# Filter spectra with their even/odd sum and difference formed by TensorE, one store per side, and the second layer's modulation blocks emitted between the filter pairs

## The chip, the core and the metric

The kernel is one program on 1 core of a Trainium2 chip. The time is device microseconds (us) of that core for one execution. Engines are named as in the profile: PE is TensorE's matmul, PEld its weight load, DVE VectorE, ACT ScalarE, POOL GpSimd, and SP the engine that issues most DMAs.

## What is computed

A two-layer trunk over 1024 tokens of width 1024 with a context of 256 tokens. Layer 0 mixes neighbourhood attention and a gated DeltaNet, layer 1 is an order-2 Hyena block. Three pieces of the reference lie around the change. The modulation vectors of both layers come from the conditioning alone, and the filters of layer 1 come from a small network alone, so both are computed at the very start, beside layer 0's input:

```python
def adaln_in(s, cvec, norm_g, mod_w, mod_b):
    m = jax.nn.silu(cvec) @ mod_w + mod_b
    shift, scale, gate = jnp.split(m, 3, axis=-1)
    return rmsnorm(s, norm_g) * (1.0 + scale) + shift, gate

def long_conv(u, h_fwd, h_bwd, skip):
    ...
    hf = jnp.fft.rfft(h_fwd, n=n, axis=0)
    hb = jnp.fft.rfft(h_bwd, n=n, axis=0)
    ...

def hyena_layer(...):
    h, gate = adaln_in(s, cvec, norm_g, mod_w, mod_b)
    ...
    filt = hyena_filters(s.shape[1], fw1, fb1, ff1, fw2, fb2, ff2, fw3)
    z = x1 * long_conv(v, filt[:, 0, 0], filt[:, 0, 1], skip[0])
    y = x2 * long_conv(z, filt[:, 1, 0], filt[:, 1, 1], skip[1])
```

## The kernel before

`start` (L328) is the first stage. It makes the filters' hidden layer, the eight shift and scale blocks of layer 0's modulation (`mod_block`, tiles em_w, em_ps, em_t), and then loops over 8 column blocks `cb`. Each round calls `filter_pair`, which makes four filters of 1024 samples for 128 channels (matmuls into fh, L1280 and L1281; DVE multiplies them by a decay at L1282; ACT squares and scales them). For each of the two orders it then runs `filter_block` one step late through `flush(0)`, and `filter_spectrum` another step late through `flush(1)`. There are so 16 spectra, and they are called filters 1 to 16 here.

`filter_block` adds and subtracts the forward and the backward filter (fp on POOL at L1304, fh on DVE at L1305) and folds the result into short pieces: ft_sd, ft_d and ff, on POOL and DVE, L1139 to L1160 and L1318. PE transposes the pieces (fx_ps, L121), and ACT copies them to fx.

`filter_spectrum` (L1323) multiplies the pieces by small DFT matrices. It does so for two sides, the sine side 1 first and then the cosine side 0. On each side the even and the odd half of the coarse piece are two matmuls of 128x256 into one PSUM tile e (profile name fb). ACT copies the even half to t (profile name fo, L1340), and DVE forms sum and difference of the two halves (L1341, L1342) in the staging tile G. DVE then adds and subtracts a second PSUM tile r to a part of that result (L1343, L1344), and ACT copies the rest of r (L1345). G holds both sides and has one buffer. When side 0 is done, two stores take it to g_d: 1 MB at L1350 and 64 KB at L1351. PSUM tiles e, r and b2 share three buffers.

Beside the filters the stage has work that a scheduler places: at `cb` 0 the code emits, with a priority below all other work, the four gate blocks of layer 0's modulation, the first halves of eight gate projections (`zblock`, PE tiles z, 24 matmuls each, 192 in all) and all twelve blocks of layer 1's modulation (j = 0 to 11). Each modulation block loads two pieces of 512 KB (om_w, L208), makes 8 matmuls into a PSUM tile om_ps, and copies it by ACT to om_p. Blocks 0 to 7 are then transposed (om_t) and reduced by DVE; blocks 8 to 11, the gate part, take a one-row matmul (om_g, L224), an addition on DVE (L227) to a row loaded for it (om_gr, L226), and a store of that row (gate_d, L228). The PSUM pool of om_ps, om_t, om_g and z has one buffer. The weights of z and of the modulation go through the same three tags, wraw, whi and wlo, with two buffers each, so that a load waits for the matmuls of six pieces earlier.

After the loop `layer0_in` transposes the second half of the tokens (xtp, L401). `load_ab` loads the small weights wab through wraw as well, and `project` begins: 48 small matmuls (ab, L574) and then the large projections (dn, L110 to L112) with weights wdn.

A scheduler sets the order of the instructions of each engine from the program, its dependencies, its own costs and the priorities; on the chip each engine then runs its list in that order. SP's list is a queue too: an issue that waits for a buffer holds what stands behind it.

## Time and profile before

| | us |
|---|---|
| median of 3 runs | 1918.72 (1909.53 to 1919.75) |
| profiled execution, its own time | 1915.67 |
| span of the profile | 1913.7 |
| granted TensorE clock, mean | 0.953 |
| PE, DVE, ACT, POOL busy | 1743.7, 1379.5, 853.8, 624.6 |
| mean DMA rate | 142 GB/s |

The busy times are sums over stages with different limits. The first stage ends where the first dn matmul starts, 387 us into the span. Within it the 16 stores at L1350 mark the ends of the filters: the first is issued at 96.3 us, the twelfth at 324.8 us and the last at 377.4 us.

### The profile page before, as it was taken

Reading aid. Unit: us, or ns where it says so; the run is one execution under the profiler, and the core shown is the slowest. Engines: PE = TensorE matmul, PEld = TensorE weight load, DVE = VectorE, ACT = ScalarE, POOL = GpSimd, SP = SyncE. Lnnn points to the kernel's source line nnn. Section 1 sums busy time; section 2 is a strip of 40 time slices with the busy share of each in tenths; the row PEclk is TensorE's granted clock in tenths of the full one; section 3 lists DMA queues with packets and bytes.
Section 4 is the critical chain, followed back from the end, with each engine's and each line's share of the span. In section 5 each row is a group of like instructions: output and inputs, shape, how many; then the busy total and the mean of one; then the engine's idle time right before and its main releaser. Section 6 shows DMA issues by size and latency. Waiting matters only on the chain. (4 is left out here: it accounts for less than half of the span.)

```text
span 1913.7 us, 30399 instructions
## 1 busy us (share of the span) xinstructions
PE 1743.7 (91%) x11156; PEld 1422.0 (74%) x11156; DVE 1379.5 (72%) x2786; ACT 853.8 (45%) x1851; POOL 624.6 (33%) x878
## 2 busy tenths in 40 slices
PE   6798988799987998999988999888999999999998
PEld 2466755688876786888866787677888888888776
DVE  5999988657648544655565665748898998898666
ACT  5566564445525342333343544544344444444421
POOL 0755554412395767811044301420000000000310
PEclk9799978899999998999998999999999999999999
DMA  8445544313434367534389854533442443444424
GB/s 303 162 131 142 171 159 160 121 45 108 142 104 122 128 202 230 174 103 158 142 236 236 233 172 105 181 94 81 111 121 72 101 124 81 123 111 112 126 104 135
DMA packets 132080, 271.05 MB, mean 142 GB/s; under 512 B 43946, under 2 KB 65978, under 8 KB 129883
## 3 DMA queue, kind: packets, MB, share of 16 engines
q1 hardware_dynamic: 122330, 233.45, 37.8%
q0 software_dynamic: 9600, 35.66, 9.9%
q8 instruction: 88, 1.44, 0.3%
q14 instruction: 62, 0.50, 0.1%
HBM read 193.03 MB, written 76.03 MB: 141 GB/s over the span
## 5 line engine op out<-in xcount | busy, mean ns | idle before, releaser
L116 PE MATMUL hx<-h1h,w1x_hi 128*128 128x512 f32 x256 | 101.2, 395 | 0.0
L112 PE MATMUL dn<-hh,wdn_lo 128*128 128x512 f32 (+1 forms) x256 | 95.6, 375 | 5.9 <-POOL wdn_lo L105 5.9
L116 PE MATMUL hx<-h1l,w1x_hi 128*128 128x512 f32 x256 | 100.9, 394 | 0.0
L652 DVE SCALAR_TENSOR_TENSOR dacc<-dpad,convw,dacc 128x1024 f32<-128x1024 f32 (+1 forms) x80 | 83.8, 1078 | 23.6 <-ACT dacc L650 19.3
L116 PE MATMUL hx<-h1h,w1x_lo 128*128 128x512 f32 x256 | 100.7, 393 | 0.0
L111 PE MATMUL dn<-hl,wdn_hi 128*128 128x512 f32 (+1 forms) x256 | 95.2, 372 | 0.0
L110 PE MATMUL dn<-hh,wdn_hi 128*128 128x512 f32 (+1 forms) x256 | 95.2, 372 | 0.0
L757 POOL TENSOR_TENSOR Xb<-Xb,sub 80x31 f32<-80x31 f32 (+15 forms) x124 | 86.3, 696 | 8.4
L755 POOL TENSOR_TENSOR sub<-Lb,Xb 80x31 f32<-80x31 f32 (+15 forms) x124 | 76.0, 613 | 35.0 <-DMA Lb<-lsc_d 21.0
L1051 ACT ACTIVATE pr<-pr,st 128x640 f32<-128x640 f32 (+1 forms) x64 | 51.4, 802 | 63.6 <-DVE st L1050 63.5
L112 PEld LDWEIGHTS dn<-hh,wdn_lo 128*128 128x128 f32 x256 | 49.1, 192 | 14.7 <-POOL wdn_lo L105 6.1
L1171 ACT COPY fx<-fx_ps 128x512 f32<-128x512 f32 (+1 forms) x96 | 43.5, 483 | 28.4 <-PE fx_ps L121 24.9
L116 PE MATMUL hu<-h1h,w1u_lo 128*128 128x512 f32 x128 | 51.3, 401 | 4.7 <-DMA w1u_lo<-in_w 4.7
L110 PEld LDWEIGHTS dn<-hh,wdn_hi 128*128 128x128 f32 x256 | 49.2, 192 | 7.8
L121 PE MATMUL fx_ps<-ident,ff 128*128 128x128 f32 x288 | 49.9, 300 | 5.6 <-ACT fx L1171 3.6
L111 PEld LDWEIGHTS dn<-hl,wdn_hi 128*128 128x128 f32 x256 | 49.0, 192 | 8.0 <-issue 0.5
L116 PEld LDWEIGHTS hx<-h1h,w1x_lo 128*128 128x128 f32 x256 | 48.1, 188 | 9.0
L116 PEld LDWEIGHTS hx<-h1h,w1x_hi 128*128 128x128 f32 x256 | 48.2, 188 | 8.9
L116 PEld LDWEIGHTS hx<-h1l,w1x_hi 128*128 128x128 f32 x256 | 48.1, 188 | 8.9
L156 POOL DMA_DIRECT2D w1x_lo<-in_w x16 | 13.8, 864 | 124.8 <-ACT w1x_lo L154 116.7
L1280 PE MATMUL fh<-fhh,w3s 128*128 128x512 f32 x64 | 37.2, 584 | 16.6 <-DVE fh L1282 16.5
L116 PE MATMUL hu<-h1h,w1u_hi 128*128 128x512 f32 x128 | 51.5, 402 | 0.8 <-ACT hpu L1632 0.8
(571 smaller groups left out, 5967.4 us busy)
## 6 DMA issues: line engine op xcount, KB each, us to landing
hG<-g_d SPq DMA_DIRECT2D x16, 1088.0 KB
g_d<-G SPq DMA_DIRECT2D x16, 1024.0 KB
em_w<-in_em_w SPq DMA_DIRECT2D x24, 512.0 KB
om_w<-in_om_w SPq DMA_DIRECT2D x24, 512.0 KB
wz_raw<-in_w0z SPq DMA_DIRECT2D x16, 512.0 KB
w1x_raw<-in_w SPq DMA_DIRECT2D x16, 512.0 KB
w1x_lo<-in_w POOLq DMA_DIRECT2D x16, 512.0 KB, 8.0
wdn_raw<-in_w0dn SPq DMA_DIRECT2D x12, 512.0 KB
```

What stands on the lines that cost most here:

```text
L110: nc.tensor.matmul(ps, wh, xh, start=start, stop=False)
L111: nc.tensor.matmul(ps, wh, xl, start=False, stop=False)
L112: nc.tensor.matmul(ps, wl, xh, start=False, stop=stop)
L116: ins = self.nc.tensor.matmul(*args, **kw)
L121: ins = self.nc.tensor.transpose(out, x, self.ident)
L156: nc.gpsimd.dma_start(lo, src, accum_op=ALU.add)
L652: nc.vector.scalar_tensor_tensor(acc[:, t0:t0 + n], pad[:, o + j:o + j + n], cw[:, blk, j:j + 1], acc[:, t0:t0 + n], ALU.mult, ALU.add)
L755: nc.gpsimd.tensor_tensor(tv, Lb[:, j + 1:, j:j + 1].broadcast_to([80, m, c]), Xb[:, j:j + 1, 0:c].broadcast_to([80, m, c]), ALU.mult)
L757: nc.gpsimd.tensor_tensor(Xb[:, j + 1:, 0:c], Xb[:, j + 1:, 0:c], tv, ALU.subtract)
L1051: nc.scalar.activation(pr[:, :n], pr[:, :n], AF.Exp, bias=st[:, 0:1], scale=-1.0, accum_out=st[:, 1:2])
L1171: nc.scalar.copy(out[:, j0:j0 + m, :].rearrange("p a b -> p (a b)"), ps[:, :m * P])
L1280: nc.tensor.matmul(ps, ws[:, od, :], hh[:, sl], start=True, stop=False)
```

## The change

In `filter_spectrum` PE forms sum and difference itself: each half of e takes two matmuls that accumulate in PSUM, the even half and the odd half, the second time with a negated copy of the odd matrix. Those copies are made once in `filter_setup`. ACT copies the two finished parts, one to t and one to G, and DVE keeps only the two operations with r. G is one tile per side, with one buffer each, and each side is stored on its own, 512 KB, with the 64 KB row of side 0 apart. In `start` the twelve blocks of layer 1's modulation are emitted two per round from round 2 on, after `filter_pair` and with usual priority.

```diff
+OM_AT = 4
@@ start
                         for zb in Z_EARLY:
                             self.zblock(h, zb, (0,), add=True)
-                        for j in range(12):
-                            self.mod_block(mp, "om", j, self.cols1, self.gate_d[1:2, :])
...
                 self.filter_pair(cb, w3.pop(0), fil, pst, psp, psf, fw)
+
+                for j in range(2 * cb - OM_AT, 2 * cb - OM_AT + 2):
+                    if 0 <= j < 12:
+                        self.mod_block(mp, "om", j, self.cols1, self.gate_d[1:2, :])
@@ filter_setup
+        for name in ("a1", "b1"):
+            mats[name + "n"] = fc.tile([P, 1, P], F32, name=f"dft_{name}n")
+            nc.scalar.activation(mats[name + "n"], mats[name], AF.Copy, scale=-1.0)
@@ filter_spectrum
-        G = fw.tile([P, 2, 10, P], F32, name="G" + nm, tag="G", bufs=1)
...
-            self.dft([e[:, 0]], mats[m0], [xT[:, 0:2, :]])
-            self.dft([e[:, 1]], mats[m1], [xT[:, 2:4, :]])
+            for i, m in enumerate((m1, m1 + "n")):
+                self.mm(e[:, i], mats[m0][:, 0, :], xT[:, 0:2, :], start=True, stop=False)
+                self.mm(e[:, i], mats[m][:, 0, :], xT[:, 2:4, :], start=False, stop=True)
...
+            Gs = fw.tile([P, 9 - side, P], F32, name=f"G{nm}_{side}", tag=f"G{side}", bufs=1)
             t = fw.tile([P, 2, P], F32, name=f"fo{nm}_{side}", tag="fo", bufs=1)
-            Gs = G[:, side]
-            nc.scalar.copy(t, e[:, 0])
-            v.tensor_tensor(Gs[:, 4::4, :], t, e[:, 1], ALU.add)
-            v.tensor_tensor(Gs[:, 5::4, :], t, e[:, 1], ALU.subtract)
-            v.tensor_tensor(Gs[:, 0:2, :], Gs[:, 8:10, :], r[:, 0:2], ALU.add)
-            v.tensor_tensor(Gs[:, 2:4, :], Gs[:, 8:10, :], r[:, 0:2], ALU.subtract)
+            nc.scalar.copy(t, e[:, :, 1])
+            nc.scalar.copy(Gs[:, 4:6, :], e[:, :, 0])
+            v.tensor_tensor(Gs[:, 0:2, :], t, r[:, 0:2], ALU.add)
+            v.tensor_tensor(Gs[:, 2:4, :], t, r[:, 0:2], ALU.subtract)
             nc.scalar.copy(Gs[:, 6:8, :], r[:, 2:4])
...
-        nc.sync.dma_start(self.g_d[o, cb][:, 0:16, :].rearrange("p (a b) c -> p a b c", a=2), G[:, :, 0:8, :])
-        nc.sync.dma_start(self.g_d[o, cb][:, 16, :], G[:, 0, 8, :])
+            nc.sync.dma_start(self.g_d[o, cb][:, 8 * side:8 * side + 8, :], Gs[:, 0:8, :])
+            if side == 0:
+                nc.sync.dma_start(self.g_d[o, cb][:, 16, :], Gs[:, 8, :])
```

What the change does to the order is seen at three places. The first is PE's list where the eight z projections end and layer 1's modulation begins (z7 is the last projection, om_ps0 the first block; in the name of an fh tile the first figure is the round `cb`, the second the filter in it). Before:

```order
L110 MATMUL z7_0_877<-hh0_189,wz7_0_hi_872 128x512
L111 MATMUL z7_0_877<-hl0_190,wz7_0_hi_872 128x512
L112 MATMUL z7_0_877<-hh0_189,wz7_0_lo_873 128x512
...
L1280 MATMUL fh5_3_1_2740<-fhh_199,w3s_5_2571 128x512
L1281 MATMUL fh5_3_1_2740<-fhl_200,w3s_5_2571 128x512
L121 MATMUL fx4_0_0_ps4_2517<-ident_63,ff4_0_0_2498 128x128 x4
L210 MATMUL om_ps0_906<-om_w0_907,cT_159 32x256 x4
L210 MATMUL om_ps0_906<-om_w1_913,cT_159 32x256 x4
```

Now:

```order
L117 MATMUL fb05_1_1_3123<-fx5_1_1_2930,dft_b0_275 128x256
L117 MATMUL fb05_1_1_3123<-fx5_1_1_2930,dft_b1_277 128x256
L117 MATMUL fb05_1_1_3123<-fx5_1_1_2930,dft_b0_275 128x256
L117 MATMUL fb05_1_1_3123<-fx5_1_1_2930,dft_b1n_291 128x256
L111 MATMUL z7_0_881<-hh0_189,wz7_0_hi_876 128x512
L112 MATMUL z7_0_881<-hl0_190,wz7_0_hi_876 128x512
L113 MATMUL z7_0_881<-hh0_189,wz7_0_lo_877 128x512
...
L1286 MATMUL fh7_2_1_3376<-fhh_199,w3s_7_3214 128x512
L1287 MATMUL fh7_2_1_3376<-fhl_200,w3s_7_3214 128x512
L211 MATMUL om_ps0_1671<-om_w0_1672,cT_159 32x256 x4
L211 MATMUL om_ps0_1671<-om_w1_1678,cT_159 32x256 x4
```

The last z matmul stood in round 5 and stands in round 7 now; the first modulation block moves from the end of round 5 to the middle of round 7, behind all eight projections as before, and four matmuls of 128x256 stand where two did.

The second place is PE's list from the last filter's last matmuls (fb27) to the first small projection (ab0). Before, they touch:

```order
L116 MATMUL fb17_1_0_3702<-fx7_1_0_3545,dft_co_279 128x128 x4
L116 MATMUL fb17_1_0_3702<-fx7_1_0_3545,dft_a0_271 128x128
L116 MATMUL fb17_1_0_3702<-fx7_1_0_3545,dft_cc_283 128x128 x2
L116 MATMUL fb27_1_3719<-fx7_1_0_3545,dft_ccn_287 128x128 x2
L574 MATMUL ab0_3768<-hh0_189,wab_3734 32x512
```

Now, with the transposes of x left out but the first of a group:

```order
L117 MATMUL fb27_1_3787<-fx7_1_0_3605,dft_ccn_287 128x128 x2
L211 MATMUL om_ps7_2805<-om_w14_2806,cT_159 32x256 x4
L211 MATMUL om_ps7_2805<-om_w15_2812,cT_159 32x256 x4
L404 MATMUL xtp1_3_3701<-ident_63,x0_4_2831 128x128
...
L211 MATMUL om_ps8_3170<-om_w17_3177,cT_159 32x256 x4
...
L225 MATMUL om_g8_3185<-om_p8_3183,sel_164 1x256
L404 MATMUL xtp1_7_3737<-ident_63,x0_4_2831 128x128
...
L211 MATMUL om_ps9_3191<-om_w18_3192,cT_159 32x256 x4
L211 MATMUL om_ps9_3191<-om_w19_3198,cT_159 32x256 x4
L225 MATMUL om_g9_3206<-om_p9_3204,sel_164 1x256
L577 MATMUL ab0_3836<-hh0_189,wab_3802 32x512
```

Blocks 7, 8 and 9 and the transposes of xtp 3 to 7 now stand between the last filter and ab; blocks 10 and 11 follow among the ab matmuls, ahead of the first dn.

The third place is SP's queue around the load of wab. Before:

```order
L208 DMA om_w23_1131<-in_om_w 128x1024
L226 DMA om_gr8_1078<-in_om_brow 1x256
L228 DMA gate_d_71<-om_gr8_1078 1x256
L557 DMA wab_raw_3732<-in_w0ab 128x128
L1350 DMA g_d_70<-G5_1_3159 128x2x1024
```

Now:

```order
L209 DMA om_w23_3546<-in_om_w 128x1024 [waits DMAHW7_49,PE_49]
L227 DMA om_gr8_3187<-in_om_brow 1x256 [waits DMAHW0_49,Activation_49]
L426 DMA masks_3828<-in_masks 128x384 [waits DMAHW1_49]
L430 DMA convw_3832<-in_dn_conv 128x60 [waits DMAHW2_49]
L588 DMA alog_3905<-in_a_log 128x8 [waits DMAHW3_49]
L589 DMA dtb_3906<-in_dt_bias 128x8 [waits DMAHW4_49]
L625 DMA gsr_3951<-in_gsel 40x8 [waits DMAHW5_49,Pool_49]
L229 DMA gate_d_71<-om_gr8_3187 1x256 [waits DMAHW6_49,DVE_49]
L560 DMA wab_raw_3800<-in_w0ab 128x128 [waits DMAHW7_49,PE_49]
L227 DMA om_gr9_3208<-in_om_brow 1x256 [waits DMAHW6_49,DMAHW0_49]
```

The order among om_w23, the row of block 8, its store and wab is the old one, but before, the store of filter 12 follows and four filters were still to come; now the last filter has been stored ahead of these rows, and five small loads have come in between.

## Rows read from the trace of the kernel before

**Rows 1.** The page's first part: busy us of each engine over the span.

```profile
PE 1743.7 (91%) x11156; PEld 1422.0 (74%) x11156; DVE 1379.5 (72%) x2786; ACT 853.8 (45%) x1851; POOL 624.6 (33%) x878
```

**Rows 2.** Busy time by stretch; then the granted clock, DMA share and rate.

```profile
96.00:322.00 226.00, 201.78 (x1119) 147.65 (x1112) 206.63 (x466) 136.08 (x259) 118.10 (x147) 0.89 0.51 156
322.00:377.00 55.00, 43.30 (x298) 34.48 (x297) 41.10 (x88) 24.34 (x55) 26.86 (x26) 0.87 0.29 102
377.00:387.00 10.00, 10.00 (x55) 5.84 (x54) 0.87 (x3) 1.80 (x5) 1.08 (x8) 1.00 0.40 135
```

**Rows 3.** Who waited for whom, 96 to 387 us, PE: total, times, longest.

```profile
PE fh L1280 <- DVE fh L1282: 12.8, 6, 3.5
PE fb L116 <- DVE G L1342: 10.3, 6, 2.9
PE fb L116 <- ACT G L1345: 3.8, 2, 3.5
```

**Rows 4.** Groups of instructions, 40 to 384 us, DVE: busy us, mean ns.

```profile
L1140 DVE TENSOR_TENSOR ft_sd<-fh 128x512 f32<-128x512 f32 x16 | 20.6, 1286 | 0.0
...
L1341 DVE TENSOR_TENSOR G<-fo,fb 128x256 f32<-128x256 f32 x32 | 13.1, 410 | 6.9 <-DMA g_d<-G 6.6 <-ACT fo L1340 0.3
```

**Rows 5.** Timeline of DVE: start us, us, instruction.

```profile
188.00 0.41 DVE L1341 TENSOR_TENSOR G<-fo,fb 128x256 f32<-128x256 f32 x1
188.33 0.41 DVE L1342 TENSOR_TENSOR G<-fo,fb 128x256 f32<-128x256 f32 x1
...
189.26 0.68 DVE L1140 TENSOR_TENSOR ft_sd<-fh 128x512 f32<-128x512 f32 x1
...
195.06 2.40 DVE L1160 TENSOR_TENSOR ff<-ft_d 128x128 f32<-128x128 f32 x1
...
198.32 0.41 DVE L1344 TENSOR_TENSOR G<-G,fb 128x256 f32<-128x256 f32 x1
```

**Rows 6.** Timeline of POOL in the same stretch.

```profile
194.69 2.62 POOL L1304 TENSOR_TENSOR fp<-fh,fh 128x1024 f32<-128x1024 f32 x1
...
197.35 1.27 POOL L1139 TENSOR_TENSOR ft_sd<-fp 128x512 f32<-128x512 f32 x1
```

**Rows 7.** Timeline of PE around filters 11 and 12.

```profile
299.95 1.06 PE L116 MATMUL fb<-fx,dft_so 128*128 128x128 f32 x8
...
301.51 1.03 PE L116 MATMUL fb<-fx,dft_a 128*128 128x256 f32 x4
302.38 0.71 PE L121 MATMUL fx_ps<-ident,ff 128*128 128x128 f32 x5
303.02 1.07 PE L210 MATMUL om_ps<-om_w,cT 128*32 128x256 f32 x16
...
309.04 2.08 PE L116 MATMUL fb<-fx,dft_co 128*128 128x128 f32 x8 [2.89 <-DVE G L1342]
...
327.76 0.59 PE L224 MATMUL om_g<-om_p,sel 128*1 128x256 f32 x2
```

**Rows 8.** Timeline of PE, the first ab and the first dn matmul.

```profile
376.65 0.56 PE L574 MATMUL ab<-hh,wab 128*32 128x512 f32 x1
...
387.16 0.40 PE L110 MATMUL dn<-hh,wdn_hi 128*128 128x512 f32 x1
```

**Rows 9.** Who waited for whom, 336 to 387 us, DVE.

```profile
DVE G L1341 <- DMA g_d<-G: 6.6, 2, 5.3
```

**Rows 10.** Timeline of SP's DMA issues.

```profile
324.33 0.35 SPq L557 DMA_DIRECT2D wab_raw<-in_w0ab  x1
...
378.39 0.92 SPq L423 DMA_DIRECT2D masks<-in_masks  x1
...
381.68 0.32 SPq L622 DMA_DIRECT2D gsr<-in_gsel  x1
```

**Rows 11.** Tile wab: duration ns min/median/max, first and last start us.

```profile
L102 ACT CAST wab<-wab_raw x1: 298/298/298, 326.2 to 326.2; 128x128 fp32r<-128x128 f32 x1
L105 DVE TENSOR_TENSOR wab<-wab_raw,wab x1: 272/272/272, 327.7 to 327.7; 128x128 fp32r<-128x128 f32 x1
```

More of the change, by code (lines that the diff above doesn't have):

```diff
@@ L1348, in filter_spectrum @@
                 self.dft([b2], mats["ccn"], [xT[:, 6, :], xT[:, 8, :]])
-                nc.scalar.copy(G[:, 0, 8, :], b2)
-        nc.sync.dma_start(self.g_d[o, cb][:, 0:16, :].rearrange("p (a b) c -> p a b c", a=2), G[:, :, 0:8, :])
-        nc.sync.dma_start(self.g_d[o, cb][:, 16, :], G[:, 0, 8, :])
+                nc.scalar.copy(Gs[:, 8, :], b2)
+            nc.sync.dma_start(self.g_d[o, cb][:, 8 * side:8 * side + 8, :], Gs[:, 0:8, :])
+            if side == 0:
+                nc.sync.dma_start(self.g_d[o, cb][:, 16, :], Gs[:, 8, :])
     def load_wout(self, w, pool, ap, name, gate, order, lo_eng=(None,), ahead=0):
```

## The prediction

> **What bounds the kernel now.** I read the busy times of the whole span first. PE leads with 91% [rows 1], but that is a mean over stages, so I cut the first stage out of the span, which alone is touched. The table by stretch shows three parts [rows 2]. In A, 96 to 322 us, where filters 1 to 12 run, DVE is busy 206.6 of 226 us (91%), and PE is busy 201.8 us at a granted clock of 0.89: both are nearly full. In B, 322 to 377 us, where the last four filters run out, neither is full (PE 43.3, DVE 41.1 of 55). In C, 377 to 387 us, PE is full with ab, and then the dn matmuls begin. What shifts the first dn shifts the end, since PE goes on without a gap there. So the question is when the first dn matmul starts; now it is 387.16 us [rows 8].
>
> Next I read what PE waits for: 12.8 us for the filters' products on DVE, 10.3 us for DVE to release tile e, and 3.8 us for an ACT copy [rows 3]. A wait costs more than its length. After 2.89 us of it eight matmuls of 128x128 took 2.08 us, against 1.06 us for the same number elsewhere [rows 7]: the granted clock was at its lower level, 1.2 instead of 2.4 GHz. A mean of 0.89 is the lower level in 22% of the time.
>
> Last I read how DVE and POOL stand together. A DVE subtraction of 128x128 took 2.40 us and ended at 197.46, just after POOL's fp operation (194.69 to 197.31) [rows 5, 6]. An operation of 128x512 that took 0.68 us at 189.26 has a mean of 1.286 us in its group [rows 4, 5]. But the G operation at 198.32 took its usual 0.41 us inside POOL's work from 197.35 to 198.62 [rows 5, 6]. Operations on two SBUF tiles so wait for POOL, and those that read PSUM do not. Part of DVE's busy time is this waiting.
>
> **Part A: filters 1 to 12.** The change removes two DVE operations per side, four per filter, 48 in A. One is 0.41 us long, but the next starts after 0.33 us [rows 5], so 48 x 0.33 = 15.8 us leave DVE. They are the kind that runs beside POOL, and POOL is busy 118.1 of 226 us, 52% [rows 2]. What is freed in that share is likely to be spent waiting for POOL, so I keep 48% of it, 7.6 us. The ends are 15.8 us (nothing lost) and 3 us (PE fuller, see next).
>
> The Trainium skill (page "SBUF — State Buffer", section "SBUF: two separate sides") describes a port pair that DVE and GpSimd lock against each other, which a DVE operation takes with two SBUF inputs. This trace agrees in the two operations just named; by that rule the removed operations cost less than their length and the sum is the one taken here, and without it A would be 8.2 us better and the sum 4 us below the time of before.
>
> PE gets four matmuls of 128x256 more per filter. Four trace entries of that form (two matmuls, each entered twice) occupy PE from 301.51 to 302.38 us, so one matmul is 0.43 us and a filter 1.74 us, 20.9 us in A [rows 7]. The modulation blocks go out of A: by the order the first follows the last z in round 7, where it followed in round 5. About nine of twelve leave, at 1.0 us for om_ps plus some 0.25 us for its transposes, 11 us. PE so has 10 us more work in A. It has 24 us of idle time there, and up to 25 us are lost to the lower clock (22% of 226 us at half speed), so this fits. What helps PE is that tile e is now released by two ACT copies and not by DVE, which is the late engine: the wait of 10.3 us [rows 3] should go, with the slow matmuls after it. I count 4 us for it, since in most of A DVE is the later of the two. ACT gets 24 copies more, about 8 us, and is busy 136 of 226 us [rows 2]; that is hidden, and costs up to 8 us if PE waits for each. The two negated matrices, made once, cost nothing beside the loads before the first filter. **A: -12 us, between -22 and -3.**
>
> **Part B: the last four filters.** DVE waits 6.6 us here, once 5.3 us, for the 1 MB store of G before it may write G again [rows 9]. A tile per side, stored as soon as that side is done, removes this; the side written next was stored half a filter earlier. What is late next is the chain of the last filter itself (scaling, folds, transposes, matmuls), so I count 5 us. Against it stand 4 x 1.74 = 7 us of matmuls, and blocks 1 to 6 of the modulation in place of blocks 9 to 11, some 3 us, less 2.2 us of transposes of x that move behind the last filter: 7.5 us more for PE, which idles 11.7 us and runs at 0.87 [rows 2]. Most fits into the gaps; I count 5 us. **B: 0 us, between -6 and +6.**
>
> **Part C: from the last filter to the first dn.** Today this is 387.16 - 376.65 = 10.5 us of ab alone [rows 8]. The order puts five modulation blocks there, 5 x 1.0 us (om_ps: 303.02 to the next start is a little over 1 us [rows 7]), three one-row matmuls ahead of dn, 3 x 0.52 us, five groups of four transposes, 2.2 us, and a pair for block 7, 0.2 us. That is **9.0 us** of PE work with nothing beside it.
>
> Then there is a wait that was not there. wab is loaded behind om_w23, the row of block 8 and its store in SP's list. Before, it was issued at 324.33 us, 52 us ahead of its use [rows 8, 10]. Now om_w23 cannot be issued until block 8's second half has run, since it takes its buffer. From there: two issues 0.7 us; the five small loads from masks to gsr, which took from 378.39 to 382.00, 3.6 us [rows 10]; the gate store's and wab's issues 0.6 us; landing 1.9 us (324.33 to the cast at 326.2); cast 0.3 us and subtraction 0.27 us [rows 10, 11]. That is 7.4 us less 0.3 us that overlap, 7.1 us. PE has 2.9 us to do meanwhile (two groups of transposes 0.9, block 9's 1.0, two one-row matmuls 1.0) and stands still for **4.2 us**. Behind it the ab matmuls stand in the queue, and through them the first dn. After a gap of 2.89 us the clock was low [rows 7], which I put at **2.5 us** more. **C: +16 us, between +9 (work alone) and +28 (the second rival).**
>
> **The sum** is -12 + 0 + 16 = +4 us on the profiled execution's 1915.67 us, 1919.7 us, so I say **1920 us**. The median of the runs shown is 3.05 us above that execution, well inside their scatter of 10 us, and I add nothing for it. That is no change: 0.5%, 9.6 us, is about what a measurement of this kernel can tell.
>
> **Rival 1, faster.** DVE alone sets A, and the freed time is kept in full: A is -22 us (15.8 + 6 for e), B -6, C +9 because wab lands in time. The sum is -19 us, **1897 us**. For it speak DVE's 91% in A and the waits of PE for DVE, which lead its list [rows 2, 3]; against it the half of DVE's time in which POOL works, and that the order moves modulation work to where nothing covers it.
>
> **Rival 2, slower.** One queue decides: SP's, between block 8 and ab. If the issue of the gate store and of wab must wait until om_w22 and om_w23, 1 MB, have landed (the longest wait for 1 MB was 5.3 us [rows 9]), and block 10 in the middle of ab must wait for row 9, which is loaded only after the store of row 8 has landed (two small transfers of 1.9 us each, as wab's), the stall is 4.2 + 5.3 + 3.8 = 13.3 us and the lower clock after it some 5.5 us. C is then +28, and the sum -12 + 0 + 28 = +16 us, **1931 us**. It decides from a C above 21.6 us on, that is, from 12.6 us of stall and slow clock. For it speaks the order of SP's list, which holds these issues in a row; against it that the om_w loads were never what PE waited for before [rows 3].
>
> That the change doesn't do what it says is half certain: no modulation block can start before the eight z are through, so they are not spread over the rounds; this is in the sum.
>
> **How the numbers follow.** I give the forecast 0.40, rival 1 0.32, rival 2 0.28. Its signs come from these: faster 0.32, same 0.40, slower 0.28. The forecast's own range is 1910 to 1928 us. For 8 in 10 the range must hold most of both rivals: 1896 to 1938 us, which leaves out about half of rival 1's lower side and the worst of rival 2.
>
> **What would show it.** In the profile after, DVE should have 64 operations of L1341's kind fewer and each filter four dft_a and dft_b matmuls of 128x256 on a side; PE's wait for DVE's release of e should be gone; the last filter's store should come near 365 us rather than 377.4, and the first dn about 27 us after the last filter's matmuls, at some 391 us. PE should show a gap of 3 to 5 us before the first ab, with wab's load as its releaser. The forecast is wrong if the last filter ends before 357 us (A kept in full), or if the first dn comes more than 32 us after the last filter.

## The result, and the profile after

The changed kernel took 1923.45 us (median of 11 runs, 1919.86 to 1929.5) against 1918.33 us for the kernel before in the same session (11 runs, 1909.53 to 1920.55): a ratio of 1.0035, 95% interval 1.0023 to 1.0048. That is 0.35% slower, inside the 0.5% that was called no change. The profiled execution took 1922.6 us, with a span of 1920.8 us against 1913.7 before.

In the changed kernel's file the lines of the functions touched stand 1 to 8 further down than in the rows of before (L110 is L111, L1343 is L1350, L574 is L577; L1341 and L1342 are gone).

The page's first part answers to [rows 1]: DVE has 64 operations fewer, PE 128 entries more (64 matmuls, each entered twice).

```profile
PE 1757.7 (92%) x11284; PEld 1435.1 (75%) x11284; DVE 1367.9 (71%) x2722; ACT 863.0 (45%) x1885; POOL 619.9 (32%) x878
```

The busy time by stretch, with the stretches cut at about the same places in the program as in [rows 2] (near the end of filter 12, after the last filter, at the first dn):

```profile
96.00:307.00 211.00, 194.04 (x1026) 151.03 (x1025) 186.36 (x394) 135.42 (x267) 109.70 (x134) 0.94 0.42 125
307.00:364.00 57.00, 50.62 (x390) 41.29 (x388) 39.31 (x82) 26.84 (x68) 23.25 (x29) 0.94 0.60 206
364.00:396.40 32.40, 25.65 (x179) 12.88 (x177) 9.97 (x22) 9.20 (x20) 6.74 (x12) 0.84 0.35 113
```

Part A became 15 us shorter by these cuts (12.5 us by the start of the first matmul behind filter 12, 320.29 before and 307.81 after), B is about as long as it was, and C grew from 10 to 32 us. In A, PE's granted clock rose from 0.89 to 0.94. In C, PE is busy for 25.65 of 32.40 us only, at 0.84, where it was full at 1.00.

What PE waits for between 96 and 397 us, in the columns of [rows 3]: the 10.3 us for DVE to release tile e are gone; 7.0 us for ACT's copies of tiles r (L1352) and b2 (L1356), which share their three buffers with e, stand where there were 3.8 (L1345). The second row has grown to 5.5 us.

```profile
PE fh L1286 <- DVE fh L1288: 9.4, 7, 4.0
PE om_ps L211 <- DVE om_gr L228: 5.5, 1, 5.5
...
PE fb L117 <- ACT G L1356: 5.0, 3, 4.4
PE fb L117 <- ACT G L1352: 2.0, 2, 1.3
...
PE ab L577 <- DVE wab L106: 0.4, 1, 0.4
```

Before, between 96 and 387 us, the second row read:

```profile
PE om_ps L210 <- DVE om_gr L227: 0.9, 1, 0.9
```

The longer wait is one gap in C. The timeline of PE from the last filter's end to the first dn, which answers to [rows 8]:

```profile
363.51 0.61 PE L117 MATMUL fb<-fx,dft_ccn 128*128 128x128 f32 x4
...
367.20 1.07 PE L211 MATMUL om_ps<-om_w,cT 128*32 128x256 f32 x16
...
369.34 0.66 PE L404 MATMUL xtp<-ident,x 128*128 128x128 f32 x4
375.51 1.94 PE L211 MATMUL om_ps<-om_w,cT 128*32 128x256 f32 x16 [5.52 <-DVE om_gr L228]
...
379.45 0.63 PE L577 MATMUL ab<-hh,wab 128*32 128x512 f32 x1 [0.44 <-DVE wab L106]
379.88 0.63 PE L577 MATMUL ab<-hl,wab 128*32 128x512 f32 x1
...
384.67 0.39 PE L577 MATMUL ab<-hl,wab 128*32 128x512 f32 x1
...
394.85 1.07 PE L211 MATMUL om_ps<-om_w,cT 128*32 128x256 f32 x16
...
396.40 0.50 PE L111 MATMUL dn<-hh,wdn_hi 128*128 128x512 f32 x1
```

At 369.99 us PE has run out of work: block 9's om_ps needs the one PSUM buffer that block 8's gate products hold until DVE has added block 8's row to them. Behind the gap the clock is low: a block takes 1.94 us where it takes 1.07, and ab matmuls start every 0.43 us until 384.14, every 0.23 us from then on. SP's issues and DVE's list up to the addition show what the gap waited for:

```profile
367.90 0.95 SPq L209 DMA_DIRECT2D om_w<-in_om_w  x2
368.94 0.32 SPq L227 DMA_DIRECT2D om_gr<-in_om_brow  x1
...
375.48 0.24 SPq L229 DMA_DIRECT2D gate_d<-om_gr  x1
376.65 0.35 SPq L560 DMA_DIRECT2D wab_raw<-in_w0ab  x1
```

```profile
372.65 0.69 DVE L106 TENSOR_TENSOR hl<-xmod,hh 128x512 fp32r<-128x512 f32 x1 [0.69 <-ACT hh L103]
375.05 0.41 DVE L228 TENSOR_TENSOR om_gr<-om_gr,om_g 1x256 f32<-1x256 f32 x1 [1.70 <-DMA om_gr<-in_om_brow]
```

The row of block 8 is 1 KB, issued at 368.94 right behind two loads of 1 MB together, and DVE has it at 375.05, 6.1 us later. The row is the last of two things that the addition waits for: until 373.34 us DVE goes through the operations on the modulated x (xmod, hl) that stand ahead of the addition in its list, and only the 1.70 us behind that are the row's alone. wab's load is issued only behind the gate store of that row, but then it delays ab by 0.44 us only.

For the experiments I cut each profiled execution at the first fb matmul of the first filter (it starts between 81.6 and 86.3 us in the executions, before anything that the change touches), at the end of the last filter's matmuls and at the first dn; "rest" is the span less the start of the first dn. All times are us; the ratio is that of the runs to the runs of before on the same chip. One profiled execution stands for each kernel. In those that leave z in its place and let nothing wait behind the first dn, "rest" already lies between 1523.5 and 1527.6 us, so a difference of some 4 us in it tells nothing.

| kernel | ratio [95%] | filters | tail | filters + tail | rest |
|---|---|---|---|---|---|
| before | 1 | 295.3 | 10.2 | 305.5 | 1526.5 |
| changed | 1.0035 [1.0023, 1.0048] | 281.1 | 32.3 | 313.4 | 1524.4 |
| spectra only | 1.0066 [1.0038, 1.0094] | 272.1 | 42.6 | 314.7 | 1527.6 |
| emission only | 0.9985 [0.9964, 1.0005] | 295.4 | 10.9 | 306.3 | 1525.2 |
| blocks ahead of z | 1.0133 [1.0081, 1.0185] | 277.5 | 52.5 | 330.1 | 1530.7 |
| two matmuls a side | 0.9960 [0.9942, 0.9978] | 271.5 | 26.0 | 297.5 | 1526.9 |
| two z blocks moved | 0.9984 [0.9968, 1.0000] | 276.2 | 21.3 | 297.5 | 1528.0 |
| second PSUM buffer | 1.0182 [1.0148, 1.0216] | 315.3 | 16.6 | 331.9 | 1526.4 |
| wab early | 1.0049 [1.0025, 1.0073] | 279.7 | 25.6 | 305.3 | 1530.9 |
| one tile | 0.9980 [0.9958, 1.0002] | 277.8 | 21.2 | 299.1 | 1525.1 |
| before, store split | 1.0032 [1.0014, 1.0049] | 290.0 | 17.6 | 307.6 | 1523.5 |
| before, two z moved | 0.9977 [0.9963, 0.9991] | 282.4 | 10.2 | 292.6 | 1531.9 |
| one tile, two z moved | 0.9964 [0.9943, 0.9984] | 277.9 | 18.9 | 296.8 | 1524.0 |
| one tile, three z moved | 0.9956 [0.9943, 0.9969] | 274.1 | 18.4 | 292.5 | 1534.8 |

### The profile page after: what moved, and what is told of

The parts are those of the page before. It is cut to its first block, busy times and chain, and to the rows that moved or that the text cites. A ratio compares the mean times of both kernels' runs of the same rounds, so it can differ in the third digit from the quotient of the medians.

```text
span 1920.8 us, 30658 instructions
## 1 busy us (share of the span) xinstructions
PE 1757.7 (92%) x11284; PEld 1435.1 (75%) x11284; DVE 1367.9 (71%) x2722; ACT 863.0 (45%) x1885; POOL 619.9 (32%) x878
## 5 line engine op out<-in xcount | busy, mean ns | idle before, releaser
L111 PE MATMUL dn<-hh,wdn_hi 128*128 128x512 f32 (+1 forms) x256 | 95.3, 372 | 0.0
L111 PEld LDWEIGHTS dn<-hh,wdn_hi 128*128 128x128 f32 x256 | 49.0, 191 | 7.7
L122 PE MATMUL pt<-ident,pr 128*128 128x128 f32 x304 | 46.6, 279 | 6.1 <-DVE pts L1067 5.0
```

Source lines behind the costliest of these rows:

```text
L111: nc.tensor.matmul(ps, wh, xh, start=start, stop=False)
L122: ins = self.nc.tensor.transpose(out, x, self.ident)
```

## The experiments

My theory behind the result was that the new matmuls fill PE's gaps in the filters, that the fill work with low priority (z, then the blocks of the second layer's modulation) therefore ends later, and that what is left of it behind the last filter runs uncovered. Rivals: the place where the blocks are emitted, the single PSUM buffer, SP's queue, the split of the store.

**Spectra only.** The butterflies and stores of the change, the blocks emitted as before.

```diff
+                        for j in range(12):
+                            self.mod_block(mp, "om", j, self.cols1, self.gate_d[1:2, :])
...
-                for j in range(2 * cb - OM_AT, 2 * cb - OM_AT + 2):
-                    if 0 <= j < 12:
-                        self.mod_block(mp, "om", j, self.cols1, self.gate_d[1:2, :])
```

> The new spectra and stores, with layer 1's modulation emitted at round 0 with low priority as before. Theory (the extra matmuls fill the gaps of TensorE in which the z projections and the modulation used to run, so the blocks come late whatever the place of their emission): the same as the whole change, 1923 us within 5, with the first dn near 396 us and five or so modulation blocks behind the last filter. Rival (the new place of emission put the blocks at the end): the filters' gain of 12 us is kept and the end of the stage goes back to its old 10.5 us, so 1906 us within 5, first dn near 375 us.

Measured: 1931.99 us (1921.47 to 1935.67). Neither range held it, and the theory's sign was right. The blocks start at 298.61 us, as late as in the changed kernel (301.9), so they are late whatever emits them. The tail is 42.6 us, with seven of the blocks in it instead of five. The emission between the pairs is the smaller evil of the two: with it, filters and tail are 313.4 instead of 314.7 us in the profiles, and the ratio is lower by 0.3%, though the intervals overlap.

**Emission only.** The spectra, the tile and the stores of before, the blocks emitted between the pairs.

```diff
+OM_AT = 4
...
-                        for j in range(12):
-                            self.mod_block(mp, "om", j, self.cols1, self.gate_d[1:2, :])
...
+                for j in range(2 * cb - OM_AT, 2 * cb - OM_AT + 2):
+                    if 0 <= j < 12:
+                        self.mod_block(mp, "om", j, self.cols1, self.gate_d[1:2, :])
```

> The old spectra and stores, with layer 1's modulation emitted between the pairs. Theory: nothing moves, since the blocks can't start before the z projections are through, which end where they ended: 1918 us within 4, first dn near 387 us. Rival (emission between the pairs puts blocks behind the last filter): slower by 8 us or more, 1926 us or above, first dn at 395 us or later.

Measured: 1913.31 us, 0.7 us below the theory's range and far from the rival's; a ratio whose interval holds 1, and a stage within 1 us of before in both parts. The second half of the change does nothing by itself: the blocks go behind z either way, and z ends at 239 us here, as before (233).

**Blocks ahead of z.** If the blocks' chain of loads and additions made the tail, it should help to run them first and leave z to the end.

```diff
+                        for j in range(12):
+                            self.mod_block(mp, "om", j, self.cols1, self.gate_d[1:2, :])
                         for zb in Z_EARLY:
...
-                for j in range(2 * cb - OM_AT, 2 * cb - OM_AT + 2):
-                    if 0 <= j < 12:
-                        self.mod_block(mp, "om", j, self.cols1, self.gate_d[1:2, :])
```

> The new spectra and stores, with all twelve modulation blocks emitted at round 0 ahead of the z projections, both with low priority; what is late is then z, long rows of matmuls that wait for nothing. Theory (the end of the stage is long because of the modulation's chain of waits): TensorE has no gap of 5 us before ab, the clock stays high, and the first dn starts near 386 us: 1913 us within 5. Rival (only the amount of TensorE's work counts): first dn stays near 396 us, 1923 us within 5.

Measured: 1943.36 us (4 runs). Both ranges missed. Now z is what stands behind the last filter (it runs to 413.8 us), the tail is 52.5 us, and z itself waits for the single buffer (between 86 and 417 us; 5.5 us of it in the tail):

```profile
PE z L111 <- DVE zt L488: 10.0, 4, 4.5
```

So the blocks' chain is not what makes a tail long: with z in it PE is busy 45.0 of 52.5 us, against 25.5 of 32.3 in the changed kernel. What grew is the work left there, and the idle time is about the same.

**Two matmuls a side.** This leaves out the two matmuls that bring the second half of the input into the sum and the difference (its spectra are not the reference's); copies and stores stay.

```diff
-            for i, m in enumerate((m1, m1 + "n")):
-                self.mm(e[:, i], mats[m0][:, 0, :], xT[:, 0:2, :], start=True, stop=False)
-                self.mm(e[:, i], mats[m][:, 0, :], xT[:, 2:4, :], start=False, stop=True)
+            self.dft([e[:, 0]], mats[m0], [xT[:, 0:2, :]])
+            self.dft([e[:, 1]], mats[m1], [xT[:, 2:4, :]])
```

> The changed kernel with two matmuls of 128x256 per side in place of four: sum and difference of the even and odd halves are left out, the rest is as in the change. It prices the 64 added matmuls (27.8 us of TensorE at full clock). Theory: filters 1 to 12 take what they take now, within 5 us, since DVE sets them; z and the modulation come earlier by what TensorE has free, three blocks instead of five follow the last filter, 1914 us within 6. Rival (the added matmuls are hidden): 1923 us within 4. Second rival (TensorE is the limit of the filters now): 1903 us or less, with the last filter ending before 352 us.

Measured: 1910.3 us, and three blocks behind the last filter, as the theory has it. One part of it failed: filter 12 ends 10.1 us earlier, counted from the first fb matmul, where 5 at most were allowed for, so in the changed kernel DVE alone does not set that stretch. The 64 added matmuls cost 0.75% or 14 us by the ratios (1.0035 against 0.9960), 9.6 us in the filters and 6.3 in the tail by the profiles. At 0.43 us each they are 27.5 us of work, so some half of them fitted into gaps. With those DVE operations gone and no matmuls added for them, filters and tail are 297.5 us, only 8.0 less than before: that is about what the move could have gained at no price (0.9960).

**Two z blocks moved.** Here the left-over work is made less by two of the eight z blocks (24 matmuls each).

```diff
-Z_EARLY = range(8)
+Z_EARLY = range(6)
```

> The changed kernel with two of the eight z blocks (24 matmuls each) computed in the projection ahead of the filters instead of as low-priority work between them; nothing else. Theory (the filters' new matmuls fill the gaps of TensorE, so z ends later and the modulation blocks are left over behind the last filter): about 11 us more before the filters (2 x 5.5 us), the modulation's blocks end before or right at the last filter, first dn 15 to 20 us after it instead of 32.4, and the time is 1912 to 1918, below the changed kernel's 1923. Rival (the uncovered work is only moved from behind the filters to ahead of them; the filters' own pace sets the rest): 1923 to 1930. Second rival (the tail's 32 us are the chain of loads on the SP queue, not left-over work): first dn stays 28 us or more after the last filter, 1927 to 1935.

Measured: 1913.8 us, inside the theory's range of time. One thing in that text is wrong: the two blocks are not computed ahead of the filters but behind them, in the projection. The tail is 21.3 us, over the 15 to 20 expected, though only one block is left in it. The stall on DVE's addition is gone; what is left are waits for DVE's modulated x (xmod), of which the changed kernel has 0.25 us there (in both, transposes of x now stand behind the last filter; before, none did):

```profile
PE xtp L404 <- DVE xmod L406: 3.9, 2, 2.5
PE om_g L225 <- ACT om_p L214: 0.5, 1, 0.5
```

The two blocks, some 11 us of matmuls, lengthen the rest by 3.6 us in these two profiles (1524.4 to 1528.0), which is not clear of its scatter.

**Second PSUM buffer.** The blocks 8 to 11 of layer 1's modulation and their gate products take their PSUM tile from the filters' pool of two.

```diff
-        ps = self.psg.tile([P, 512], F32, name=f"{name}_ps{j}", tag="g")
+        ps = (self.psg if j < 8 or name == "em" else self.psq).tile([P, 512], F32, name=f"{name}_ps{j}", tag="g")
...
-            ps = self.psg.tile([P, 512], F32, name=f"{name}_g{j}", tag="g")
+            ps = (self.psg if name == "em" else self.psq).tile([P, 512], F32, name=f"{name}_g{j}", tag="g")
...
+        self.psq = psp
```

> The changed kernel with the second layer's gate products and its gate blocks in the filters' own PSUM pool (two buffers) instead of the single buffer that z, the blocks and the products share; nothing else. Theory (the stall of 5.5 us before block 9, where it waits for VectorE's addition of block 8's row, is a wait for the single buffer, and it holds the blocks behind the last filter): that wait goes, the lower clock behind it goes too, first dn 20 to 25 us after the last filter, time 1912 to 1917. Rival (the amount of left-over work sets the tail; the buffer only decides where it stalls): first dn 29 to 33 us after the last filter, 1920 to 1925.

Measured: 1952.14 us (4 runs), 1.8% slower than before; both ranges missed by far. The wait for the addition is gone from the tail and the tail is short (16.6 us). But the order then sets most of the blocks ahead of the last two filters' products (ten of the twelve om_ps groups start between 295 and 341 us), and the stretch with the blocks and the one behind it read:

```profile
295.00:345.00 50.00, 42.45 (x364) 29.99 (x364) 18.91 (x45) 19.49 (x51) 9.90 (x16) 0.93 0.83 291
345.00:398.50 53.50, 37.98 (x194) 25.72 (x195) 36.17 (x69) 20.61 (x41) 23.31 (x19) 0.71 0.15 51
```

In the first, PE works through blocks and the filters before, and DVE has little to do (18.9 of 50 us), while the DMA queues run at 291 GB/s; in the second the last two filters run with nothing beside them, with a wait of 8.8 us for DVE's folds and a granted clock of 0.71. Fill work that is bunched ahead of the last filters is then missing beside them.

**wab early.** wab's load is issued in the filters' last round, ahead of blocks 10 and 11.

```diff
+                if cb == KT - 1:
+                    self.wab = self.load_ab()
...
-                wab = self.load_ab()
-            self.project(h, wab)
+            self.project(h, self.wab)
```

> The changed kernel with wab's load issued at the filters' last round ahead of the last two blocks, so that it isn't behind their rows and the gate store on SP's queue; the place of the multiplication is the same. The step of the prediction: a stall of 4.2 us before the first ab with wab's load as releaser. Theory: in the changed kernel that wait is 0.44 us only, so 0 to 2 us are gained: 1920 to 1924. Rival (the chain of SP's queue behind block 8 does set the tail through wab): first dn 5 us earlier or more, 1914 to 1918.

Measured: 1925.18 us, nothing gained; just above the theory's range. The profile shows more than the time does: ab starts at 374.91 and the first dn at 391.03, 5.4 us earlier than in the changed kernel, as the rival has it (8.1 us counted from the first fb), PE's wait for the addition is 0.52 us, and the tail's clock is 1.00. But most of it is given back at once. From the first dn to the next step, the transposes of k, the changed kernel and this one read:

```profile
396.40:425.49 29.09, 29.09 (x154) 24.39 (x154) 16.92 (x24) 13.91 (x23) 10.58 (x10) 1.00 0.23 73
```

```profile
391.03:425.95 34.92, 32.28 (x156) 26.77 (x153) 19.25 (x22) 13.62 (x22) 10.56 (x10) 0.90 0.21 61
```

PE is full there in the first, and idles 2.64 us at a clock of 0.90 in the second: the last block's gate products and the gates of the layer now come late behind the first dn. The transposes begin at 425.5 and 425.9 us; counted from the first fb, 5.8 of the 8.1 us are gone by then. The stall was for the most part moved behind the first dn, not removed.

**One tile.** The split of the tile and the store is undone, TensorE's butterflies stay.

```diff
+        G = fw.tile([P, 2, 9, P], F32, name="G" + nm, tag="G", bufs=1)
...
-            Gs = fw.tile([P, 9 - side, P], F32, name=f"G{nm}_{side}", tag=f"G{side}", bufs=1)
+            Gs = G[:, side]
...
-            nc.sync.dma_start(self.g_d[o, cb][:, 8 * side:8 * side + 8, :], Gs[:, 0:8, :])
-            if side == 0:
-                nc.sync.dma_start(self.g_d[o, cb][:, 16, :], Gs[:, 8, :])
+        nc.sync.dma_start(self.g_d[o, cb][:, 0:16, :].rearrange("p (a b) c -> p a b c", a=2), G[:, :, 0:8, :])
+        nc.sync.dma_start(self.g_d[o, cb][:, 16, :], G[:, 0, 8, :])
```

> The changed kernel with one spectra tile and the two stores of the kernel before instead of a tile and a store per side; the butterflies stay on TensorE. It prices the part of the change that splits the store. Theory (the wait for the store of the filter before, 6.6 us in the kernel before, goes because each side's copies wait for their own side's store only): 5 to 12 us slower than the changed kernel, 1928 to 1935. Rival (the store was never on the filters' path): 1921 to 1925.

Measured: 1911.96 us. Both missed; it is faster by 0.55% or 10.5 us than the changed kernel. The waits for the store are there again, on ACT (first row) and DVE:

```profile
ACT G L1350 <- DMA g_d<-G: 11.3, 6, 3.2
```

```profile
DVE G L1351 <- DMA g_d<-G: 4.0, 2, 3.0
```

But PE does not feel them: the filters take 277.8 us, not more than with two tiles (281.1). What differs is the order on PE. The last z is at 278.7 us instead of 297.6, and the first block of the modulation at 285.5 instead of 301.9, so that less is left behind the last filter and PE's wait for the addition is 1.69 us, and the ab matmuls behind it keep the full clock:

```profile
364.01 0.59 PE L225 MATMUL om_g<-om_p,sel 128*1 128x256 f32 x2
...
371.08 1.07 PE L211 MATMUL om_ps<-om_w,cT 128*32 128x256 f32 x16 [1.69 <-DVE om_gr L228]
372.08 0.41 PE L577 MATMUL ab<-hh,wab 128*32 128x512 f32 x1
372.33 0.40 PE L577 MATMUL ab<-hl,wab 128*32 128x512 f32 x1
```

Why the plan sets z earlier here was not tried. It may count the store's wait as a gap and fill it; that is argued, not shown.

**Before, store split.** The kernel before with a tile and a store per side.

```diff
-        G = fw.tile([P, 2, 10, P], F32, name="G" + nm, tag="G", bufs=1)
...
-            Gs = G[:, side]
+            Gs = fw.tile([P, 10, P], F32, name=f"G{nm}_{side}", tag=f"G{side}", bufs=1)
...
-        nc.sync.dma_start(self.g_d[o, cb][:, 0:16, :].rearrange("p (a b) c -> p a b c", a=2), G[:, :, 0:8, :])
-        nc.sync.dma_start(self.g_d[o, cb][:, 16, :], G[:, 0, 8, :])
+            nc.sync.dma_start(self.g_d[o, cb][:, 8 * side:8 * side + 8, :], Gs[:, 0:8, :])
+            if side == 0:
+                nc.sync.dma_start(self.g_d[o, cb][:, 16, :], Gs[:, 8, :])
```

> The kernel before with its VectorE butterflies, and a tile and a store per side as the changed kernel has them; the blocks are emitted as before. It prices the split of the store by itself, because the changed kernel without it ran at 1912. Theory (the split is worth nothing by itself on the filters' path; what costs is which fill work is left over behind the last filter, and here only the last of the blocks is): first dn 300 to 308 us after the first filter's first fb (305.5 before), 1914 to 1922. Rival (the split itself costs the 10 us that lie between the changed kernel and the same with one tile): 1924 to 1930.

Measured: 1919.52 us, inside the theory's range (the rival's begins at 1924). But the interval of the ratio lies above 1, so the theory's "worth nothing" does not hold: by itself the split costs 0.32% (0.14 to 0.49), some 6 us. The split shortens the filters by 5.3 us (295.3 to 290.0) and the tail takes back 7.4 (10.2 to 17.6): the last block runs to the end of the filters (its om_ps start at 374.43, before at 339.53). The same trade as in the change, with one of its parts alone. On either kernel the split delays the fill work: counted from the first fb, the first block of the modulation starts 11.8 us later here than before (168.7 for 156.9), and 19.7 us later in the changed kernel than in "one tile" (218.9 for 199.3).

**Before, two z blocks moved.**

```diff
-Z_EARLY = range(8)
+Z_EARLY = range(6)
```

> The kernel before with two of the eight z blocks left to the projection behind the filters: the control for the same move on the changed kernel (1913.8 against about 1922). The expectation of that run said the blocks go ahead of the filters; they are computed behind them, in the projection, where the two blocks lengthened the time from the first dn to the end by 3.6 us only (1524.4 to 1528.0). Theory (the move gains only where blocks are left over behind the last filter; before, none are, and VectorE sets the filters' pace): 10 us from the last filter to the first dn as before, 1913 to 1921. Rival (the move gains by itself, whatever the spectra do): 1904 to 1911.

Measured: 1912.25 us, 0.23% faster than before. The lower end of the theory's range missed it by 0.75 us and the upper end of the rival's by 1.25, so both are in part right: the move is worth 0.23% on the kernel before and 0.51% on the changed one (1.0035 to 0.9984). So about half of what it gave the changed kernel comes by itself (filters 282.4 for 295.3, rest 1531.9 for 1526.5). The other half goes with the tail, which is 10.2 us in both here and 21.3 for 32.3 there.

**One tile and fewer z blocks.** The edit of "one tile", with Z_EARLY = range(6), and with range(5).

> The changed kernel with one spectra tile and the two stores of before, and two z blocks left to the projection: both edits that gained, together. Theory (both gain by the same thing, fewer blocks left over behind the last filter, so their gains don't add up in full; one block's end is left there): 12 to 20 us from the last filter to the first dn, 1904 to 1911. Rival (with one edit the stall is gone already and the second brings nothing): 1911 to 1916.

> The same with three z blocks left to the projection; by the order on TensorE no block is then left behind the last filter. Theory: 10 to 14 us from the last filter to the first dn, filters 6 to 10 us shorter than with one tile alone, 2 to 6 us more in the projection: 1902 to 1910. Rival (the filters without the fill run at VectorE's and ScalarE's pace and are not shortened, and the third block costs its full 5.5 us behind them): 1912 to 1918.

Measured: 1908.99 and 1909.28 us, ratios 0.9964 and 0.9956, inside the theories' ranges of time. With three blocks moved the rest of the theory failed: the filters are 3.8 us shorter than with one tile alone and not 6 to 10, and the tail is 18.4 us and not 10 to 14, though no modulation block is left in it. Transposes of x are, and PE waits for DVE's xmod between them four times:

```profile
PE xtp L404 <- DVE xmod L406: 3.1, 4, 0.9
```

Behind them the first ab matmuls again start only every 0.43 us. So left-over blocks are not the whole of a tail. The gains overlap, as expected: from one tile alone (0.9980) a second edit brings some 0.2%, which the intervals do not separate. The third z block buys 4.3 us in filters and tail in its profile; what it costs in the rest (1534.8) cannot be told, since the profiled execution, 1914.95 us, is the slowest of its nine. By the medians the two end at the same time. These two are the fastest versions found, 0.4% or 8 us faster than before (less than the 0.5% named above, though the intervals lie below 1) and 0.75% below the changed kernel. They are not separated from the kernel before with two z blocks moved (0.9977), so nothing here shows that TensorE's butterflies gain anything once z is placed well.

## Why the prediction was right, and where it was not

The forecast was 1920 us and no change; the runs say 1923.45 and 0.35% slower. On the profiled executions the sum of +4 us was +9.2 us at the first dn (387.16 to 396.40) and +7.1 us of span.

- **Part A, -12 us: right in size, for another reason.** By the end of filter 12 it was -12.5. That the two agree is luck: the loss to POOL that was counted did not come, and the new matmuls, which were taken to fit into gaps, took 10.1 us ("two matmuls a side"). Of the freed 15.8 us of DVE I kept 48%, since the rest was to be lost to waits for POOL. Over the filters, DVE's folds on SBUF tiles (seven groups, equal counts) took 108.5 us before and 108.2 after: no time was lost to POOL that had not been lost before, and DVE's busy time there fell from 259.7 to 236.6 us. Three of those groups between 96 and 322 us, the kind of [rows 4]:

```profile
L1163 DVE TENSOR_TENSOR ff<-ft_sd 128x256 f32<-128x256 f32 x23 | 20.4, 885 | 0.0
L1163 DVE TENSOR_TENSOR ff<-fh 128x512 f32<-128x512 f32 x12 | 16.3, 1359 | 8.2 <-PE fx_ps L122 8.2
L1143 DVE TENSOR_TENSOR ft_sd<-fh 128x512 f32<-128x512 f32 x12 | 14.6, 1219 | 0.0
```

In the same view of before the same three took 697, 1263 and 1309 ns each. So the discount that I took beside the shared port pair of the Trainium skill (page "SBUF — State Buffer", section "SBUF: two separate sides") is not what held A: single operations are long beside POOL, but their sum did not grow. What held A is PE's own new work: without the 64 matmuls the filters take 271.5 us, 9.6 us less. The wait for DVE's release of e went, as predicted, and the clock rose (0.89 to 0.94), though no run prices the 4 us counted for it.

- **Part B, 0 us: right in sum; its terms are not shown.** From filter 12's end to the last filter's end it was 56.7 us before and is 56.3 after. PE's added work was summed as 7.5 us, its terms give 7.8; 5 were counted either way. The store of [rows 9] no longer holds DVE. But the split of the store, counted at -5 us, brings the whole kernel no gain: by itself it costs 0.32% ("before, store split"), and the change without it is 0.55% faster ("one tile"). That it delays the fill work was not in the sum.

- **Part C, +16 us: the step that was mis-sized; it was +22.1** (10.2 to 32.3), inside its bounds of 9 and 28. The work with nothing beside it was counted at 9.0 us, and its five blocks, three one-row matmuls and five groups of transposes are all there. Left out were two groups of ab's transposes, 1.5 us, that ran between the dn matmuls before and now run ahead of the first. The stall was counted at 4.2 us and is 6.75 (32.40 - 25.65), of which 5.52 in one place, and the lower clock behind it at 2.5 us and is some 3.8: the stretch from 375.5 to 384.1 was granted half the clock throughout, with 7.60 us busy. With the 9.0 us of work these terms make some 21 of the 22.1 us.

```profile
375.50:384.10 8.60, 7.60 (x29) 2.56 (x30) 0.80 (x3) 0.88 (x3) 0.18 (x1) 0.50 0.04 10
```

The wrong step is the place. I put the stall ahead of the first ab, with wab's load as its releaser. It is one step earlier: block 9's om_ps waits for DVE to add block 8's row, because z, blocks and gate products share a single PSUM buffer. Of the 5.52 us the row accounts for the last 1.70, since its 1 KB took 6.1 us behind 1 MB of om_w; up to there DVE was at x's modulation, which the prediction did not count in the tail either. I had taken 1.9 us for a small transfer, from a quiet moment of wab's load. wab itself then cost 0.44 us, since its chain ran while PE worked on block 9 at the lower clock. "wab early" cures this link, and most of the stall then stands behind the first dn.

- **Rival 2** (one queue decides, from a C above 21.6 us on): C reached its point by half a microsecond, and its mechanism, a small row behind 1 MB on its way, is the one that the trace shows, though for the row of block 8 and not for wab and block 10. It had two such rows cost a wait each; the trace shows one.

- **Rival 1** (DVE sets A, its time is kept in full): fell with A. With the added matmuls left out ("two matmuls a side") A comes out as this rival had it: counted from the first fb, filter 12 ends 23.9 us earlier than before. But the tail then gives 15.8 back, and filters and tail are 8.0 us shorter, not 19. Over filters and tail PE's busy time went from 266.9 to 282.3 us (+15.4) and its idle time from 38.6 to 31.1 (-7.5); the difference, +7.9, is the change's price (305.5 to 313.4). DVE's busy time fell by 14.2 us in the same stretch; that this bought the 7.5 is argued, not shown.

- Of what the text said the profile would show, these came: 64 DVE operations fewer; the wait for e gone; the last filter's end near 365 (its last matmul ends at 364.1). The first dn came 32.3 us after it, past the 32 that were to show the forecast wrong, at 396.4 and not 391; the gap's releaser was the row.

Which part of the change makes it slower has no single answer: leaving out the 64 matmuls brings it below the time before (0.9960), and so, by its median, does leaving out the split alone (0.9980, the interval holds 1). What stays open: why two tiles make the plan put z 19 us later than one tile does, and how much of the 10.5 us between these two is that order and how much the wait and the clock in the tail. The tail is 11.1 us of the profiles' difference of 14.3.

## What to carry to other kernels

When work is moved to an engine that a scheduler also uses for fill work, price not only the stage it is moved into but the fill work that it displaces: ask where the last of it ends, and what covers it there. A buffer or a load that is harmless while other work stands in the queue becomes the bound when the same steps run alone, and to cure one link of such a chain can move the stall to the next; taking work out of the stage (here two z blocks, worth 0.51% on the changed kernel and 0.23% on the one before) helped. Once an order is set by a plan, an edit that looks neutral (one tile or two) can be worth more than the edit one means to measure, so take the parts of a change apart before crediting any of them.

## What was not expected of the hardware

- A gap of PE can cost more than its length: after 1.69 us of waiting ("one tile") the ab matmuls started every 0.23 to 0.25 us, after 5.52 us (the changed kernel) every 0.43 us for 4.7 us, which is the lower of the two levels. And work that fills gaps costs less than its length: the 27.5 us of matmuls that "two matmuls a side" leaves out lengthened filters and tail by 15.9 us (297.5 to 313.4), with the granted clock of the filters at 0.95 instead of 0.92.
- A load of 1 KB issued 0.09 us behind 1 MB on the same queue was usable after 6.1 us, while wab's 64 KB in a quiet moment took 1.9 us [rows 10, 11].
- A high transfer rate was no sign of progress: in "second PSUM buffer" the queues moved 291 GB/s for 50 us, about twice the rate in the changed kernel's filters (149), and the kernel was 1.8% slower.
